# A decoder stack on one core: banks of an FFN chunk from one pool, read halfway by ScalarE; other slots, ranks and listed durations

## The chip, the cores and the metric

The kernel runs on one core of a Trainium2 chip, in one launch. The metric is device time in microseconds (us), the median over executions. The engines are named as the profile names them: PE is TensorE's matrix multiply and PEld its weight load, DVE is VectorE, ACT is ScalarE, POOL is GpSimd, SP is SyncE, which issues nearly all DMAs here.

## The reference

Two layers over x of 256 tokens and 2048 features, all in float32. A layer has three parts, each added to x:

```python
h = rms_norm(x, attn_norm_g[l]); proj = h @ w_in[l]              # 2048 -> 4688 columns
mixed = concat([ssd_mixer(...), mla_mixer(...)]) @ w_out[l]      # state-space scan and causal attention
x = x + mixed
x = x + memory_cross_attention(rms_norm(x), rms_norm(mem), ...)  # 4 heads, 256 memory tokens
h = rms_norm(x, ffn_norm_g[l])
x = x + (silu(h @ w_gate[l]) * (h @ w_up[l])) @ w_down[l]        # hidden 5632
```

The third part, the feed-forward part (FFN), is what most of the change is about.

## The kernel before, in words

Every float32 matmul is made of three in the fast format float32r. A weight tile of 256 rows and 512 columns ("unit", `raw`) is loaded, split into `hi` (ACT rounds it) and `lo` (DVE takes the remainder, raw - hi), and the product is xh·hi + xh·lo + xl·hi. `raw`, `hi` and `lo` are buffers of one tag, `w`, which has 20. PE holds 128 rows of x as its stationary operand and streams 512 columns of weights into one PSUM bank of 512 numbers.

The eight banks are two pools: `ps_acc`, tag "acc", has four and `ps_tp`, tag "tp", has four. `gemm` takes two acc banks, one for each half of the tokens. Transposes and small products use tp.

The FFN goes over 11 column chunks of 512 hidden columns. Chunk 0 is a plain gemm for gate and one for up. Chunks 1 to 10 go through `gate_up` (L1310): parts of the rows of gate and up are combined so that seven products of 18 matmuls and two blocks of 24 do what eight products of 24 would. Sums of weights (`b11 + b12` and the like) are made by DVE in place in `raw`, some by DMA that adds (`plus`, on POOL's queue). A chunk has four banks: `q` and `f` from acc, `cg` and `cu` from tp. q collects one product after another and is read three times on the way and once at the end. `seven_rows` makes the combined rows of x ahead of the FFN.

The two halves of a chunk's result are turned by a DMA transpose (`split_T_dma`, `turn`): the tile `gg` is copied in 16-bit halves to `hs`, transposed by DMA to `ht`, copied back into `whole` (L430: gg's own memory is used again), and split into a pair of tiles dh and dl, the rows for the down product. Chunks form sections [0], [1, 2], [3, 4], ... [9, 10]. After each chunk of a section a half of the previous section's down products is made: `down` (L1383) makes 512 columns of x at a time with `gemm` and adds both accumulators to x (`add_x`, L1174). So between chunk 1 and 2, and between 2 and 3, lie two down products of 24 matmuls each; between later chunks two of 48.

Tiles of 4 KB a partition are of the tag "b4", which has 22; those of up to 2 KB of the tag "s2", which has 6.

Nothing is issued in the order of the code. Each call is recorded (`Recorder.add`) with its dependences, and `issue` (L272) sets the order by a list schedule: it walks through time with a cost for each operation (`cost`, L244) and a lag until its result is seen, takes for each engine the operation that can start first, and among equals the one of lower rank. Rank is the place in the code plus `rec.bias`: weight splits have -400, the sums of weights (`add`, L1304) -425. A tile takes a slot of its tag when its first operation is listed; tiles of a tag are numbered in the order of the code. With a margin m for its tag (L1448), a tile before which `ahead` earlier ones are still without a slot may take one only if more than min(m, ahead) are free; with m = 0, if any is. Then the operations are issued in the listed order, and on the chip each engine keeps its own in that order and waits by semaphores.

In `issue` a recorded operation is made real at L374, so every instruction has that line in the profile and is known by its tiles.

Of the kernel before, what the change touches and what calls it, by code (L numbers as in the profile page):

```python
# [8 lines left out]
F32 = mybir.dt.float32  # L9
# [8 lines left out]
P = 128  # L18
S = 256
# [169 lines left out]
class Recorder:  # L189
# [3 lines left out]
    LAG = 0.35  # L193
    DMA_LAG = 2.0
    SECOND = 0.6
# [48 lines left out]
    def cost(self, engine, method, args, kw, writes, reads):  # L244
        n = max(v.free_size() for v in reads + writes) if reads or writes else 1
        if method == "dma_start_transpose":
            return 2.2, 1.6
        if method == "dma_start":
            if "accum_op" in kw:
                return 1.3, 8.0  # L250
            if engine == "SP":
                return n * 512 / 360e3, self.DMA_LAG
            return (1.1 if engine == "Pool" else 0.1), self.DMA_LAG + 0.6
        if engine == "PE":
            n = args[0].free_size()
            if method == "transpose":
                return 0.1075, self.LAG
            passes = 1 if args[1].tile.dtype == F32R else 4
            return max(passes * n / 2400 + 0.003, 0.107), self.LAG
        ptr = sum(0.07 for v in reads if v.free_size() == 1)  # L260
        if engine == "ACT":
            return 0.09 + n * 0.833e-3 + ptr, self.LAG
        if engine == "Pool" and kw.get("op") == ALU.pow:
            return 0.3 + n * 0.165, self.LAG
        if engine == "Pool":
            return 0.15 + n * 2.2e-3, self.LAG
        fast = not any(v.tile.psum for v in reads + writes) and method in ("tensor_copy", "tensor_scalar")
        if method == "reciprocal":
            n *= 8
        return 0.065 + n * (0.52e-3 if fast else 1.04e-3) + ptr, self.LAG  # L270

# [106 lines left out]
def hybrid_kernel(ctx: ExitStack, tc: tile.TileContext, const, vec, rows, x_in, x_tr, mem, mem_tr, positions, w_in, w_q_b,  # L378
# [110 lines left out]
    def load_unit(w, r0, c0, n, pieces=1):  # L489

        if not ahead and not asked:
            return ask(w, r0, c0, n, pieces)
        key = id(w), r0, c0
        while key not in asked or (ahead and len(asked) <= 2):
            first = ahead.pop(0)
            asked[id(first[0]), first[1], first[2]] = ask(*first, 512)
        return asked.pop(key)
# [4 lines left out]

    def ask(w, r0, c0, n, pieces=1):
        raw = wpool.tile([P, 2, n], F32, tag="w", name=nm("raw"), bufs=20)
        src = w[r0:r0 + 256, c0:c0 + n].rearrange("(k p) n -> p k n", p=P)
        for i in range(pieces):
            k = slice(2 // pieces * i, 2 // pieces * (i + 1))
            SP.dma_start(raw[:, k, :], src[:, k, :])
        return raw
# [650 lines left out]
    def mem_T(l):  # L1160
# [11 lines left out]
        return mT  # L1172

    def add_x(j, accs):  # L1174
        for t in range(NT):
            xs = x[j][:, t, :]
            V.tensor_add(xs, xs, accs[t])

# [124 lines left out]

    def add(out, a, b, do=V.tensor_add):  # L1304
        rec.bias -= 425
        for o, u, v in zip(out, a, b) if isinstance(out, list) else [(out, a, b)]:
            do(o, u, v)
        rec.bias += 425

    def gate_up(wg, wu, c, x1, half, full, rstd):  # L1310
# [6 lines left out]
        c0 = 512 * c  # L1317
        q, f = acc_tile(), acc_tile()
        cg, cu = tp_tile(), tp_tile()
        gg, uu = b4([P, NT, 512], "gg"), [s2([P, 512], "uu") for _ in range(NT)]  # L1320

# [10 lines left out]
        product(q, half["a11"], [h11])  # L1332
        A.copy(gg[:, 0, :], q)

# [5 lines left out]
        product(f, half["s1"], [h11])  # L1340
        A.copy(uu[0], f)

        b22 = load_raw(wu, 1536, c0, 512)
        add(b11, b11, b22)
        add(b12, b12, b22)
        product(cu, full["s4"], b22, start=True)
        h22 = load_unit(wu, 256, c0, 512)
        add(h11, h11, h22)
        add(h12, h12, h22)
        product(cu, half["s4"], [h22])  # L1350
        product(q, full["s2"], b11)
        plus(b11, wg, 1536, c0)
        product(q, half["s2"], [h11])
        add(uu[0], uu[0], q, V.tensor_sub)

# [5 lines left out]
        product(q, full["s3"], b12)  # L1361
        product(q, half["s3"], [h12])
        mm_chunk([cu, f], x1, load_w(wu, 512, c0, 512), 512, [False] * NT, [True, True], again=True)
        A.copy(uu[1], f)
        add(uu[1], uu[1], q, V.tensor_sub)
        add(uu[0], uu[0], cu)
        mm_chunk([cg, q], x1, load_w(wg, 512, c0, 512), 512, [False] * NT, [True, False], again=True)
        add(gg[:, 0, :], gg[:, 0, :], cg)
        A.activation(gg[:, 0, :], gg[:, 0, :], AF.Silu, scale=rstd[:, 0:1])

        product(q, full["a22"], b11)
        product(q, half["a22"], [h11], stop=True)
        A.activation(gg[:, 1, :], q, AF.Silu, scale=rstd[:, 1:2])
        for t in range(NT):
            V.scalar_tensor_tensor(gg[:, t, :], uu[t], rstd[:, t:t + 1], gg[:, t, :], op0=ALU.mult, op1=ALU.mult)
        return gg

    def ffn(l, xT, rstd):
# [19 lines left out]
        for sec in sections:  # L1398
            for i, c in enumerate(sec):
                if c == 0:  # L1400
                    ahead.extend((w, r + h, 0) for w in (wg, wu) for r in FULL for h in (0, 256))
                else:
                    ahead.extend((w, r, 512 * c) for w, r in (
                        (wg, 1024), (wg, 1280), (wg, 0), (wu, 1024), (wu, 1280), (wu, 0), (wu, 1536), (wu, 1792),
                        (wu, 256), (wg, 1536), (wg, 1792), (wg, 256), (wu, 512), (wu, 768), (wg, 512), (wg, 768)))
                if before:
                    n = DC // len(sec)
                    ahead.extend((wd, 512 * r + h, 512 * j) for j in range(n * i, n * (i + 1)) for r in before
                                 for h in (0, 256))
            before = sec  # L1410
        ahead.extend((wd, 512 * r + h, 512 * j) for j in range(DC) for r in before for h in (0, 256))
        before = None
        for sec in sections:
            hT = []
            for i, c in enumerate(sec):
                if c == 0:
                    xs = [lambda i, k, t: half[f"a{t + 1}{1 + k // 2}"][:, i, k % 2, :], x1]
                    xs += [lambda i, k, t, b=b: full[f"a{t + 1}{b}"][:, i, k, :] for b in (1, 2)]
                    ag = gemm(xs, wg, FULL, 0, 512)
                    hh = b4([P, NT, 512], "gg")  # L1420
                    for t in range(NT):
                        A.activation(hh[:, t, :], ag[t], AF.Silu, scale=rstd[:, t:t + 1])
                    au = gemm(xs, wu, FULL, 0, 512)
                    for t in range(NT):
                        V.scalar_tensor_tensor(hh[:, t, :], au[t], rstd[:, t:t + 1], hh[:, t, :], op0=ALU.mult,
                                               op1=ALU.mult)
# [20 lines left out]
    with tc.manual_schedule():  # L1447
        rec.issue({"b4": 6, "s2": 2, "tp": 0, "w": 99, "acc": 4})  # L1448

# [72 lines left out]
```

## Time and profile before

| | |
|---|---|
| median of 3 runs | 2264.48 us (2263.03 to 2264.68) |
| the profiled execution | 2267.05 us, of which its span is 2265.3 |
| busy, share of the span | PE 98%, PEld 81%, DVE 84%, ACT 66%, POOL 4% |
| mean granted clock of PE | 0.997 of full speed |
| DMA | 215 GB/s in the mean |

Matmuls overlap in the profile (a row lasts some 390 ns, the next starts 227 ns after it), so a busy PE is judged by its starts and by what it waits for. Waits are inferred from semaphores; a wait for several is put down to the one that came last.

### The profile page before, as it was taken

To read this page: it belongs to the slowest core of one execution; us is meant where nothing else is said; L and a number is where in the kernel's file an instruction comes from. 1 tells how busy PE (TensorE), PEld (TensorE's weight loads), DVE (VectorE), ACT (ScalarE), POOL (GpSimd) and SP (SyncE) were. 2 spreads that over 40 slices of the span, in tenths; PEclk is the share of its full clock that TensorE was granted. 3 is DMA by queue.
4 is the path that set the end of the run, shared out by engine and by line. 5 is a ranking of instruction groups with operands and counts; after the bars stand their busy time and mean duration, and the time that the engine had idled before them with its cause. 6 is when DMAs were issued, how large, how long until landed. Compare 5 with 4: busy or idle time off the path is not lost.

```text
span 2265.3 us, 29133 instructions
## 1 busy us (share of the span) xinstructions
PE 2222.9 (98%) x10118; PEld 1845.7 (81%) x10118; DVE 1910.6 (84%) x2568; ACT 1500.4 (66%) x2183; POOL 93.0 (4%) x78
## 2 busy tenths in 40 slices
PE   9999999998999999999999999999989999999999
PEld 9878878787888888888898788887878888888787
DVE  7898876789998999999778888857899999999894
ACT  7768666766766666676666686657666667666762
POOL 0001000000000000000000010000000000000000
PEclk9999999999999999999999999999999999999999
DMA  9866496676777777787777665856767777777773
GB/s 319 236 193 186 142 284 196 187 212 197 239 224 212 229 232 235 228 247 226 194 230 223 172 177 171 244 185 182 219 201 226 232 220 213 236 231 226 239 234 138
DMA packets 374515, 487.96 MB, mean 215 GB/s; under 512 B 145376, under 2 KB 168544, under 8 KB 374368
## 3 DMA queue, kind: packets, MB, share of 16 engines
q1 hardware_dynamic: 363456, 465.13, 65.1%
q0 software_dynamic: 10912, 20.98, 5.5%
q8 instruction: 79, 1.29, 0.2%
q14 instruction: 68, 0.56, 0.1%
HBM read 450.92 MB, written 2.10 MB: 200 GB/s over the span
## 4 chain that ended last, share of the span: by engine, by line
PE 71%; DVE 6%; DMA 5%; issue 2%; ACT 1%; SPq 0%; DVEq 0%; ACTq 0%
PE acc L374 59%; PE tp L374 13%; DVE lo L374 3%; DMA raw<-in_w_up_dram 1%; DVE raw L374 1%; DMA ht<-hs 1%; ACT hi L374 1%; DVE x L374 1%; DMA raw<-in_w_xv_dram 0%; DMA raw<-in_w_out_dram 0%; DMA raw<-in_w_in_dram 0%; DVE uu L374 0%; DMA raw<-in_w_gate_dram 0%; SPq L374 0%; DVE hTl L374 0%
## 5 line engine op out<-in xcount | busy, mean ns | idle before, releaser
L374 ACT CAST hi<-raw 128x1024 fp32r<-128x1024 f32 (+3 forms) x996 | 1002.7, 1034 | 559.9 <-PE acc L374 223.4
L374 DVE TENSOR_TENSOR lo<-raw,hi 128x1024 fp32r<-128x1024 f32 (+3 forms) x998 | 1167.9, 1200 | 177.3 <-ACT hi L374 125.2
L374 PE MATMUL acc<-hi,x 128*128 128x512 f32 x1392 | 373.1, 392 | 0.0
L374 PEld LDWEIGHTS acc<-hi,x 128*128 128x128 f32 x1392 | 263.4, 189 | 55.4
L374 PE MATMUL acc<-hi,xTh 128*128 128x512 f32 (+1 forms) x768 | 289.3, 377 | 0.0
L374 PE MATMUL acc<-hi,xTl 128*128 128x512 f32 (+1 forms) x768 | 289.1, 376 | 0.0
L374 DVE TENSOR_TENSOR raw<-raw,raw 128x1024 f32<-128x1024 f32 x200 | 239.2, 1221 | 50.7 <-DMA raw<-in_w_up_dram 50.2
L374 PE MATMUL acc<-hi,hTh 128*128 128x512 f32 x704 | 273.9, 389 | 0.0
L374 PE MATMUL acc<-hi,hTl 128*128 128x512 f32 x704 | 273.9, 389 | 0.0
L374 PE MATMUL acc<-lo,x 128*128 128x512 f32 x696 | 214.8, 394 | 13.2 <-DVE x L374 13.2
L374 PE MATMUL acc<-lo,xTh 128*128 128x512 f32 (+1 forms) x768 | 211.7, 378 | 6.0 <-DVE uu L374 4.2
L374 PE MATMUL acc<-lo,hTh 128*128 128x512 f32 x704 | 191.2, 390 | 1.3 <-DVE lo L374 1.3
L374 PEld LDWEIGHTS acc<-lo,xTh 128*128 128x128 f32 x768 | 140.6, 188 | 31.3 <-DVE uu L374 6.8
L374 PEld LDWEIGHTS acc<-lo,x 128*128 128x128 f32 x696 | 131.1, 190 | 42.5 <-DVE x L374 14.9
L374 PEld LDWEIGHTS acc<-hi,xTh 128*128 128x128 f32 x768 | 144.8, 189 | 23.2 <-issue 0.7
L374 PEld LDWEIGHTS acc<-hi,xTl 128*128 128x128 f32 x768 | 144.7, 188 | 23.1 <-issue 0.7
L374 PEld LDWEIGHTS acc<-lo,hTh 128*128 128x128 f32 x704 | 131.8, 188 | 30.1 <-DVE lo L374 3.0
L374 PEld LDWEIGHTS acc<-hi,hTh 128*128 128x128 f32 x704 | 132.1, 188 | 27.5
L374 PEld LDWEIGHTS acc<-hi,hTl 128*128 128x128 f32 x704 | 132.1, 188 | 27.4
L374 PE MATMUL tp<-hi,x 128*128 128x512 f32 x480 | 128.6, 390 | 0.0
L374 DVE TENSOR_TENSOR x<-x,acc 128x512 f32<-128x512 f32 x128 | 83.5, 682 | 32.5 <-PE acc L374 32.4
L374 PEld LDWEIGHTS tp<-hi,x 128*128 128x128 f32 x480 | 90.1, 188 | 19.2
(306 smaller groups left out, 2781.7 us busy)
## 6 DMA issues: line engine op xcount, KB each, us to landing
raw<-in_w_gate_dram SPq DMA_DIRECT2D x176, 512.0 KB, 4.9
raw<-in_w_up_dram SPq DMA_DIRECT2D x176, 512.0 KB, 4.5
raw<-in_w_down_dram SPq DMA_DIRECT2D x176, 512.0 KB, 5.4
raw<-in_w_in_dram SPq DMA_DIRECT2D x80, 512.0 KB, 4.4
raw<-in_w_out_dram SPq DMA_DIRECT2D x64, 512.0 KB, 4.5
raw<-in_w_gate_dram POOLq DMA_DIRECT2D x40, 512.0 KB, 7.5
raw<-in_w_in_dram SPq DMA_DIRECT2D x46, 368.0 KB, 4.5
raw<-in_w_kv_b_dram SPq DMA_DIRECT2D x16, 512.0 KB, 3.9
```

The costliest lines, as they stand in the source:

```text
L374: fn(*args, **kw)
```

## The change

Six things are changed together. In `gate_up` all four banks of a chunk are tp tiles; q is copied by ACT to uu after its second and third product, and DVE subtracts that copy from f, where before ACT copied f and DVE subtracted q. `gg` becomes two s2 tiles, so the turned copy `whole` has a b4 tile of its own. The loads of rows 0 to 255 of gate and up (h11, h12) of chunks 1 to 10 get b4 tiles in place of w tiles. The sums into x use `add`, with rank -425. The list schedule has other durations and another DMA lag. The margin of tp goes from 0 to 2.

```diff
-    DMA_LAG = 2.0
+    DMA_LAG = 2.8
...
-                return n * 512 / 360e3, self.DMA_LAG
+                return n * 512 / 330e3, self.DMA_LAG
...
-            return max(passes * n / 2400 + 0.003, 0.107), self.LAG
+            return max(passes * n / 2400 + 0.0135, 0.107), self.LAG
...
-            return 0.09 + n * 0.833e-3 + ptr, self.LAG
+            return 0.17 + n * 0.833e-3 + ptr + (0.19 if "accum_out" in kw else 0.0), self.LAG
...
-        return 0.065 + n * (0.52e-3 if fast else 1.04e-3) + ptr, self.LAG
+        return 0.13 + n * (0.52e-3 if fast else 1.045e-3) + ptr, self.LAG
...
-            asked[id(first[0]), first[1], first[2]] = ask(*first, 512)
+            asked[id(first[0]), first[1], first[2]] = ask(*first[:3], 512, 1, first[3:])
...
-    def ask(w, r0, c0, n, pieces=1):
-        raw = wpool.tile([P, 2, n], F32, tag="w", name=nm("raw"), bufs=20)
+    def ask(w, r0, c0, n, pieces=1, other=False):
+        raw = b4([P, 2, n], "raw") if other else wpool.tile([P, 2, n], F32, tag="w", name=nm("raw"), bufs=20)
...
+    def add(out, a, b, do=V.tensor_add):
+        rec.bias -= 425
+        for o, u, v in zip(out, a, b) if isinstance(out, list) else [(out, a, b)]:
+            do(o, u, v)
+        rec.bias += 425
+
     def add_x(j, accs):
...
-            V.tensor_add(xs, xs, accs[t])
+            add(xs, xs, accs[t])
...
-        q, f = acc_tile(), acc_tile()
-        cg, cu = tp_tile(), tp_tile()
-        gg, uu = b4([P, NT, 512], "gg"), [s2([P, 512], "uu") for _ in range(NT)]
+        q, f, cg, cu = (tp_tile() for _ in range(4))
+        gg, uu = [[s2([P, 512], n) for _ in range(NT)] for n in ("gg", "uu")]
...
         product(f, half["s1"], [h11])
-        A.copy(uu[0], f)
 
         b22 = load_raw(wu, 1536, c0, 512)
+        product(cu, full["s4"], b22, start=True)
         add(b11, b11, b22)
         add(b12, b12, b22)
-        product(cu, full["s4"], b22, start=True)
         h22 = load_unit(wu, 256, c0, 512)
+        product(cu, half["s4"], [h22])
         add(h11, h11, h22)
         add(h12, h12, h22)
-        product(cu, half["s4"], [h22])
         product(q, full["s2"], b11)
         plus(b11, wg, 1536, c0)
         product(q, half["s2"], [h11])
-        add(uu[0], uu[0], q, V.tensor_sub)
+        A.copy(uu[0], q)
+        add(uu[0], f, uu[0], V.tensor_sub)
...
         product(q, half["s3"], [h12])
+        A.copy(uu[1], q)
         mm_chunk([cu, f], x1, load_w(wu, 512, c0, 512), 512, [False] * NT, [True, True], again=True)
-        A.copy(uu[1], f)
-        add(uu[1], uu[1], q, V.tensor_sub)
+        add(uu[1], f, uu[1], V.tensor_sub)
...
-                    ahead.extend((w, r, 512 * c) for w, r in (
+                    ahead.extend((w, r, 512 * c) + ((1,) if r == 0 else ()) for w, r in (
...
-                split_T_dma(hc, lambda t: hh[:, t, :], None, hh.rearrange("p t (u s) -> p (t u) s", s=S), (A, V))
+                split_T_dma(hc, lambda t: hh[t], None, None, (A, V))
...
-        rec.issue({"b4": 6, "s2": 2, "tp": 0, "w": 99, "acc": 4})
+        rec.issue({"b4": 6, "s2": 2, "tp": 2, "w": 99, "acc": 4})
```

The remaining lines of the diff follow from gg being two tiles.

## Rows read from the trace of the kernel before

**Rows 1.** The page, part 1: busy us, share of the span, instructions.
```profile
PE 2222.9 (98%) x10118; PEld 1845.7 (81%) x10118; DVE 1910.6 (84%) x2568; ACT 1500.4 (66%) x2183; POOL 93.0 (4%) x78
```

**Rows 2.** Chain of waits, 786 to 850: start us, us, what.
```profile
790.79 4.08 PE acc L374 x18
```

**Rows 3.** Windows: stretch, busy us by engine, PE clock, DMA share, GB/s.
```profile
437.00:592.00 155.00, 146.95 (x639) 119.91 (x638) 137.35 (x143) 103.10 (x128) 6.60 (x5) 0.98 0.66 202
592.00:1060.00 468.00, 464.06 (x2035) 381.27 (x2036) 431.33 (x411) 316.48 (x345) 20.26 (x17) 1.00 0.75 231
...
910.17:971.67 61.50, 61.49 (x271) 50.87 (x272) 56.53 (x55) 40.46 (x46) 2.42 (x2) 1.00 0.74 231
```

**Rows 4.** Waits of PE, whole span: us in total, times, longest us.
```profile
PE acc L374 <- DVE x L374: 13.2, 4, 5.7
PE tp L374 <- DVE x L374: 5.2, 4, 2.3
PE tp L374 <- DVE lo L374: 4.8, 7, 1.2
PE acc L374 <- DVE uu L374: 4.2, 6, 1.3
PE acc L374 <- DVE lo L374: 3.1, 4, 1.8
```

**Rows 5.** Timeline of PE, first layer, start of chunk 2: start us, us, instructions.
```profile
531.19 0.39 PE L374 MATMUL acc<-hi,hTl 128*128 128x512 f32 x1
537.22 1.22 PE L374 MATMUL acc<-lo,x 128*128 128x512 f32 x2 [5.64 <-DVE x L374]
538.24 1.91 PE L374 MATMUL acc<-hi,x 128*128 128x512 f32 x4
539.94 1.05 PE L374 MATMUL acc<-lo,x 128*128 128x512 f32 x2
...
543.15 1.07 PE L374 MATMUL acc<-hi,x 128*128 128x512 f32 x4
```

**Rows 6.** Timeline of PE, second layer, start of chunk 2.
```profile
1658.60 0.39 PE L374 MATMUL acc<-hi,hTl 128*128 128x512 f32 x1
1664.70 1.22 PE L374 MATMUL acc<-lo,x 128*128 128x512 f32 x2 [5.71 <-DVE x L374]
...
1669.68 0.63 PE L374 MATMUL acc<-lo,x 128*128 128x512 f32 x2
```

**Rows 7.** Timeline of DVE, 526 to 560.
```profile
536.48 2.48 DVE L374 TENSOR_TENSOR x<-x,acc 128x512 f32<-128x512 f32 x4
542.81 2.36 DVE L374 TENSOR_TENSOR lo<-raw,hi 128x1024 fp32r<-128x1024 f32 x2 [3.85 <-PE acc L374]
```

**Rows 8.** Waits of all engines, 1657 to 1690.
```profile
DVE lo L374 <- PE acc L374: 3.5, 1, 3.5
```

**Rows 9.** Groups by line and form: busy us, mean ns, idle before.
```profile
L374 DVE TENSOR_TENSOR lo<-raw,hi 128x1024 fp32r<-128x1024 f32 x932 | 1108.2, 1221 | 153.1 <-ACT hi L374 105.6 <-PE acc L374 34.8 <-issue 3.5
L374 ACT CAST hi<-raw 128x1024 fp32r<-128x1024 f32 x930 | 950.6, 1051 | 525.4 <-PE acc L374 218.0 <-DMA raw<-in_w_up_dram 68.8 <-DMA raw<-in_w_down_dram 43.7
...
L374 DVE TENSOR_TENSOR uu<-uu,acc 128x512 f32<-128x512 f32 x40 | 27.2, 681 | 0.8 <-ACT uu L374 0.8
...
L374 ACT COPY uu<-acc 128x512 f32<-128x512 f32 x40 | 23.3, 582 | 7.1 <-PE acc L374 7.0
```

**Rows 10.** Waits of SP's queue, whole span.
```profile
SPq L374 <- PE acc L374: 885.0, 410, 9.2
```

**Rows 11.** Timelines of DVE, ACT and PE between chunk 6 and chunk 7.
```profile
821.95 0.75 DVE L374 SCALAR_TENSOR_TENSOR gg<-uu,rx_y,gg 128x512 f32<-128x512 f32 x1 [1.96 <-ACT gg L374]
832.58 2.18 ACT L374 COPY hs<-gg 128x512 uint16<-128x512 uint16 x4
839.59 0.62 PE L374 MATMUL acc<-lo,x 128*128 128x512 f32 x2
```

**Rows 12.** The page, part 6: DMA issues, KB each, us to landing.
```profile
raw<-in_w_gate_dram SPq DMA_DIRECT2D x176, 512.0 KB, 4.9
```

More of the change, by code (lines that the diff above doesn't have):

```diff
@@ L1302, in plus @@
             G.dma_start(raw[h], src, accum_op=ALU.add)
[L1304 to L1308, printed above, removed]
     def gate_up(wg, wu, c, x1, half, full, rstd):
         c0 = 512 * c
-        q, f = acc_tile(), acc_tile()
-        cg, cu = tp_tile(), tp_tile()
-        gg, uu = b4([P, NT, 512], "gg"), [s2([P, 512], "uu") for _ in range(NT)]
+        q, f, cg, cu = (tp_tile() for _ in range(4))
+        gg, uu = [[s2([P, 512], n) for _ in range(NT)] for n in ("gg", "uu")]
         def product(acc, d, raw, start=False, stop=False):
@@ L1332, in gate_up @@
         product(q, half["a11"], [h11])
-        A.copy(gg[:, 0, :], q)
+        A.copy(gg[0], q)
         b12 = load_raw(wu, 1024, c0, 512)
@@ L1362, in gate_up @@
         product(q, half["s3"], [h12])
+        A.copy(uu[1], q)
         mm_chunk([cu, f], x1, load_w(wu, 512, c0, 512), 512, [False] * NT, [True, True], again=True)
-        A.copy(uu[1], f)
-        add(uu[1], uu[1], q, V.tensor_sub)
+        add(uu[1], f, uu[1], V.tensor_sub)
         add(uu[0], uu[0], cu)
         mm_chunk([cg, q], x1, load_w(wg, 512, c0, 512), 512, [False] * NT, [True, False], again=True)
-        add(gg[:, 0, :], gg[:, 0, :], cg)
-        A.activation(gg[:, 0, :], gg[:, 0, :], AF.Silu, scale=rstd[:, 0:1])
+        add(gg[0], gg[0], cg)
+        A.activation(gg[0], gg[0], AF.Silu, scale=rstd[:, 0:1])
         product(q, full["a22"], b11)
         product(q, half["a22"], [h11], stop=True)
-        A.activation(gg[:, 1, :], q, AF.Silu, scale=rstd[:, 1:2])
+        A.activation(gg[1], q, AF.Silu, scale=rstd[:, 1:2])
         for t in range(NT):
-            V.scalar_tensor_tensor(gg[:, t, :], uu[t], rstd[:, t:t + 1], gg[:, t, :], op0=ALU.mult, op1=ALU.mult)
+            V.scalar_tensor_tensor(gg[t], uu[t], rstd[:, t:t + 1], gg[t], op0=ALU.mult, op1=ALU.mult)
         return gg
@@ L1419, in ffn @@
                     ag = gemm(xs, wg, FULL, 0, 512)
-                    hh = b4([P, NT, 512], "gg")
+                    hh = [s2([P, 512], "gg") for _ in range(NT)]
                     for t in range(NT):
-                        A.activation(hh[:, t, :], ag[t], AF.Silu, scale=rstd[:, t:t + 1])
+                        A.activation(hh[t], ag[t], AF.Silu, scale=rstd[:, t:t + 1])
                     au = gemm(xs, wu, FULL, 0, 512)
                     for t in range(NT):
-                        V.scalar_tensor_tensor(hh[:, t, :], au[t], rstd[:, t:t + 1], hh[:, t, :], op0=ALU.mult,
+                        V.scalar_tensor_tensor(hh[t], au[t], rstd[:, t:t + 1], hh[t], op0=ALU.mult,
                                                op1=ALU.mult)
```

## The prediction

> **What bounds the kernel now.** Part 1 of the page comes first: TensorE (PE) has a matmul under way for 98% of the span and VectorE (DVE) is busy for 84% [rows 1]. Busy PE says little by itself, since matmuls overlap, so I went to the chain of waits for its rate: 18 matmuls of 512 columns take 4.08 us, 226.7 ns each [rows 2]. A period of the feed-forward part (FFN), one column chunk of gate and up with its share of the down product, has 7 products of 18 matmuls, two blocks of 24, and two down products of 48: 174 + 96 = 270, or 61.2 us at that rate. A measured period is 61.50 us, with DVE busy for 56.5 of it [rows 3]. So PE sets the time, DVE follows at 92%, and the kernel can only gain where PE stands still.
>
> Where it stands is in the waits of PE: 13.2 us for x's sums before it may write an acc bank, 5.2 us for x's sums before transposes into tp banks, 7.9 us for weight remainders (lo), 4.2 us for the sums in uu [rows 4]. Of the 13.2 us, two waits have 5.64 and 5.71; they lie at the same place in the two layers, where chunk 2 wants its first bank [rows 5, 6]. More is lost behind them: matmuls start 425 ns apart (538.24 to 539.94 holds four), the lower of the clock's two levels, before the rate returns [rows 5]. The windows say the same: in 437 to 592 PE lacks 8 us of busy time and the mean granted clock is 0.98; the three times longer rest of that layer's FFN lacks 4 us, at 1.00 [rows 3].
>
> **The change part by part.** The sum is made against the profiled execution: 2267.05 us, of which 2265.3 are the span. The median shown is 2264.48, 2.6 below; that is subtracted at the end.
>
> *Banks.* Chunk 2's q and f waited because acc has four banks: chunk 1's q and f, and the down products j=0 and j=1, whose sums into x come last on DVE. With q, f, cg, cu all from tp, the chunk's first product needs chunk 1's q, read by a Silu more than 10 us earlier (two down products of 24 matmuls lie between). The bank wait goes at both places. Its price from starts: 531.19 to 537.22 is 6.03 us for one matmul, 5.8 lost; then 14 matmuls take 5.93 us where 3.17 would do, 2.8 lost; 8.6 together [rows 5]. In the second layer, 5.9, and 12 matmuls in 4.98 where 2.72 would do, 2.3; 8.1 together [rows 6]. That is 16.7 us, the upper end. What is late next? DVE was working up to and through x's four sums, and stood for 3.85 us only afterwards, when PE limped and freed no weight buffers [rows 7]; in the second layer for 3.5 [rows 8]. If PE doesn't stop, a DVE that sets the pace can win only that idle time: the lower end, 7.4 us. I take 12, the middle, because DVE is not far behind: no wait of PE for lo anywhere is longer than 1.8 us [rows 4]. The other x waits on acc, 13.2 - 5.6 - 5.7 = 1.9 us, go too [rows 4]. Minus 14.
>
> *Reading q halfway by ACT.* The six waits for uu (4.2 us) are of one kind: q's third reading was a subtraction that also needed f's end, so PE could not go on with q until f was finished, copied and subtracted [rows 4]. Now a copy by ScalarE (ACT) reads q right after its product, and the block of 24 matmuls into cu and f (5.44 us) covers it; the copy has 0.58 us, the DVE operation it replaces as reader 0.68 [rows 9]. The copies stay three a chunk, the subtractions too, so no engine gets more work. Behind the copy on ACT stands the next hi, which is wanted by DVE and then PE; before it can stand a hi that waits for a buffer. Bounds: minus 4.2, if all go, and plus 35, if no reading is covered (rival D); I take minus 4, since the covers are there now.
>
> Against this stands a rule of the Trainium skill, Perfetto Trace Analysis, section Matmuls: independent groups should rotate through banks, so that one's reading overlaps the next one's matmuls, and an accumulation group targets one bank. A chunk whose q is read three times in the middle does not rotate; by the rule each reading would be exposed. The row of waits shows that q's two DVE readings a chunk cost 4.2 us over twenty chunks now, since other banks' products lie between [rows 4]. What it would cost otherwise is rival D.
>
> *x's sums rank with the weights'.* Rank moves them before the queued lo operations; no instruction is added. It matters where norms wait for x: PE's 5.2 us in four waits for transposes, 1.3 each [rows 4]. x's own sums, 0.68 each by the like uu row [rows 9], stay in that path, so 0.5 to 1 is to be had each time; and a sum put in front of a lo that is wanted sooner costs 0.68. Between minus 4 and plus 1; I take minus 2.
>
> *Slots.* gg moves to two s2 tiles (six in all; uu has the other two of a chunk), h11 and h12 to the b4 pool, and the turned copy `whole` takes a b4 of its own. w gains two of 20 buffers; SyncE's queue waits 885 us in all for PE to free such buffers [rows 10], hidden while PE is busy, so I count nothing. b4 has 22 tiles: 13 hold x's rows through the FFN (half 4, full 7 once a21 is done, x1 2), four the hidden chunks of the last section, two the present one's first. At the end of chunks 4, 6 and 8 that leaves three: dh, dl and whole stand before hs, ht and the next chunk's h11 in the pool's order, and with the margin (6) a later tile may not take a slot unless more are free than tiles stand before it. The kernel before shows the shortage: gg is complete at 822.7 and hs, which needs a slot, starts only at 832.58, near the time when the first old hidden tiles come free (24 matmuls before 839.59) [rows 11]. So I expect h11's load no sooner than the last old hidden tile's release, at 839.59 [rows 11]. Landing 4.9 us, hi 1.05, lo 1.22 make 846.8; q wants it after 12 matmuls, at 842.3 [rows 9, 11, 12]. It is 4.5 us late, unless the list lets PE do the twelve matmuls of f and of cu that need no h: 24 x 226.7 = 5.44 us of cover. The list picks what can start first, so it should. Bounds at six boundaries: 0 to 27 us; I take 0.5 each, plus 3, since the cover exceeds the lateness by one and the list counts 4.4 us for a load that takes 4.9.
>
> *The durations, tp's margin, cu's place.* They change no work, only the order: with margin 2 a later tp tile leaves banks to earlier ones, and cu's products stand in the code ahead of sums that they don't need. A matmul goes from 216 to 226.8 ns in the list (measured 226.7), a DVE operation on 1024 elements from 1.13 to 1.20 us (1.22), ACT from 0.94 to 1.02 (1.05), a load from 3.5 to 4.4 us (4.9) [rows 2, 9, 12]. All come nearer to the rows. The waits they bear on are lo's 7.9 us [rows 4]; a reshuffled list can also lose elsewhere. Minus 8 to plus 8; I take 0.
>
> *Sum.* -14 - 4 - 2 + 3 = -17: 2250.1 for an execution like the profiled one, 2247.5 after the 2.6.
>
> **The rivals.**
>
> B: DVE takes over. Without the stop, lo's become late in chunks 1 to 3, and only DVE's idle time is won: -7.4 for the banks, -1 for the rest of x, -2 for uu, +1: -9.4, 2255. For it: before chunks 2 and 3 the down products have 48 matmuls instead of 96, so DVE has less time to catch up. Against: it had 17.6 us of idle time in the 155 of that stretch [rows 3].
>
> C, on the slower side: the b4 shortage. If PE keeps its order, q waits 4.5 us at each of six boundaries: 27 us against the 20 won, +7: 2271.5. It decides from 3.3 us a boundary. For it: the wait for hs above, and the many waits on SyncE's queue, where a load that waits holds those behind it [rows 10]. Against: f's and cu's products, which are free to go first.
>
> D: exposed readings. Sixty of 0.58 us are 35, less 20 won: +15, 2279.5. By the 4.2 us measured it is unlikely. The rule of Perfetto Trace Analysis in the Trainium skill speaks for it.
>
> E: the new order gives and takes the same, or h11 eats what the banks win: 2264.5, within 4.5 us (0.2%, about what a measurement of this kernel can tell from no change).
>
> **How the numbers follow.** Forecast 0.49, B 0.17, E 0.15, C 0.16, D 0.03. Faster by over 0.2% (below 2260): forecast and B, 0.66; within: E, 0.15; slower: C and D, 0.19. The forecast's own range is 2237 to 2255. Its lower bounds together (16.7 + 1.9 + 4.2 + 4 + 8 = 34.8) give 2229.7; upwards the range takes in E and half of C: 2230 to 2271.
>
> **What would show it.** Right: no PE wait for x of over 2 us at chunk 2, the clock at its upper level there, no PE wait for uu, periods of 61.3 to 61.8. B: new waits of PE for lo between chunk 1 and 3 with DVE busy over 95%. C: at the starts of chunks 5, 7, 9 waits of PE for lo, with a load of w_gate late before them. D: waits of PE's q product for ACT's copies. The forecast is wrong if PE's idle time moves into the mixer, or if chunk 2's bank wait had been hiding a DVE lag of its own size.

## The result and the profile after

The changed kernel takes 2281.32 us (median of 8 runs, 2275.99 to 2299.03), the kernel before beside it 2264.56: a ratio of 1.0081 [1.0054, 1.0107], slower by 0.8%. The forecast was 2247.5 (2230 to 2271), faster. The profiled execution has 2282.34 us, of which 2280.6 are the span.

The page, part 1, of the kernel after (compare [rows 1]): busy us, share of the span, instructions.

```profile
PE 2238.1 (98%) x10118; PEld 1859.3 (82%) x10118; DVE 1922.5 (84%) x2578; ACT 1486.4 (65%) x2173; POOL 86.6 (4%) x78
```

The same 10118 matmuls keep PE busy for 15 us longer: some run at the lower clock. The shares are within a point of those of before and do not say where. Windows laid at the same matmuls do: first mixer, its output projection, first FFN, second output projection, second FFN. The kernel before (stretch, length, busy us of PE, PEld, DVE, ACT, POOL with counts, PE clock, DMA share, GB/s):

```profile
1.00:225.20 224.20, 221.96 (x1101) 193.36 (x1102) 190.78 (x416) 165.60 (x306) 13.68 (x11) 1.00 0.78 234
225.20:332.70 107.50, 106.60 (x512) 88.48 (x511) 84.24 (x186) 68.94 (x144) 4.45 (x4) 1.00 0.70 211
...
434.20:1131.90 697.70, 685.71 (x3003) 562.74 (x3002) 625.24 (x635) 466.11 (x537) 26.86 (x22) 1.00 0.73 222
...
1354.00:1461.20 107.20, 106.33 (x509) 87.99 (x508) 88.87 (x191) 73.84 (x152) 3.28 (x2) 1.00 0.72 211
...
1561.30:2261.00 699.70, 685.68 (x3002) 562.03 (x3001) 610.79 (x598) 447.52 (x503) 25.95 (x21) 1.00 0.71 218
```

The kernel after, the same stages:

```profile
1.00:243.50 242.50, 234.12 (x1109) 203.05 (x1109) 191.40 (x412) 169.26 (x305) 7.82 (x11) 0.95 0.74 218
243.50:353.60 110.10, 107.61 (x504) 89.11 (x505) 85.33 (x186) 70.42 (x151) 4.37 (x4) 0.98 0.70 206
...
453.50:1150.20 696.70, 686.05 (x3002) 563.18 (x3002) 632.49 (x649) 459.54 (x531) 25.74 (x22) 1.00 0.75 222
...
1368.50:1482.80 114.30, 111.36 (x522) 92.26 (x522) 91.20 (x205) 76.36 (x165) 4.12 (x2) 0.97 0.68 198
...
1582.30:2276.30 694.00, 684.64 (x3000) 561.70 (x2999) 616.40 (x606) 440.17 (x499) 24.83 (x21) 1.00 0.72 218
```

The first mixer is 18.3 us longer, 12.2 of it PE's busy time (clock 0.95) and 6.1 standing; the output projections are 2.6 and 7.1 longer. The FFNs, where the whole gain of 17 was expected, are 1.0 and 5.7 shorter.

PE's waits, kernel after, whole span (compare [rows 4]): us in total, times, longest.

```profile
PE tp L374 <- DVE lo L374: 14.9, 12, 3.9
PE tp L374 <- DVE dec L374: 3.7, 1, 3.7
...
PE tp L374 <- ACT uu L374: 2.5, 2, 1.8
...
PE tp L374 <- DVE x L374: 1.1, 2, 0.8
```

The 13.2 us of acc banks waiting for x [rows 4] are gone, and 4.1 of the 5.2 of tp. In their place lo is late (tp's part 4.8 before, 14.9 now), and a new wait for the decays (dec) has appeared in the mixer. What held PE at chunk 2 is gone; the time came back, above all, in two other places.

**First place: the decays.** Timeline of PE, kernel after:

```profile
195.17 0.39 PE L374 MATMUL acc<-hi,kvaTl 128*128 128x512 f32 x1
199.27 6.71 PE L374 MATMUL tp<-xd,dec 128*128 128x64 f32 x32 [3.71 <-DVE dec L374]
```

Windows of the kernel before, and then of the kernel after, for the stretch behind it:

```profile
200.00:220.00 20.00, 19.57 (x107) 17.66 (x106) 18.24 (x49) 18.18 (x54) 3.37 (x2) 1.00 0.95 240
```

```profile
200.00:220.00 20.00, 19.74 (x82) 18.62 (x81) 11.16 (x25) 10.28 (x19) 0.00 (x0) 0.50 0.15 43
```

PE stood 3.71 us, then ran 32 matmuls of 64 columns in one piece, and the granted clock is at its lower level (0.50 of 2.4 GHz) for all 20 us: 82 matmuls instead of 107. Why was dec late? Timeline of ACT, kernel after:

```profile
171.28 1.09 ACT L374 ACTIVATE dec<-tp 128x512 f32<-128x512 f32 x2 [2.86 <-PE tp L374]
...
195.84 0.71 ACT L374 COPY hs<-kv 128x256 uint16<-128x256 uint16 x2
196.57 1.28 ACT L374 ACT_TABLE_LOAD   x1
197.86 2.71 ACT L374 ACTIVATE dec<-dec 128x512 f32<-128x512 f32 x5
```

The first inputs were there at 171; the Exps run 26 us later, behind casts and norms of later code. In the kernel before the table load begins at 168.73 and the Exps at 170.03. The list adds TABLE_LOAD (1.3 us) to the start of an Exp when it picks ACT's next instruction, so work that could start within 1.3 us kept winning; e3 below tries that.

**Second place: chunk 1 of each FFN.** Timeline of all engines, kernel after:

```profile
508.55 2.49 POOL L374 DMA_DIRECT2D raw<-in_w_gate_dram  x2 [23.70 <-DVE lo L374]
508.73 3.77 SPq L374 DMA_TRANSPOSE ht<-hs  x1
...
523.00 2.56 ACT L374 COPY whole<-ht 128x1024 uint16<-128x1024 uint16 x2 [6.84 <-DMA ht<-hs]
...
526.67 1.23 DVE L374 TENSOR_TENSOR hTl<-whole,hTh 128x1024 fp32r<-128x1024 f32 x1 [6.38 <-ACT hTh L374]
...
530.29 1.68 PE L374 MATMUL tp<-lo,xTh 128*128 128x512 f32 x4 [3.88 <-DVE lo L374]
```

Chunk 0's transposing DMA starts 0.2 us after POOL's first adding DMA. The DMA view, 508 to 525, kernel after (busy tenths and GB/s in 40 slices; issues with KB each and median us to landing):

```profile
DMA  8886595999999999999999969981999999999999
GB/s 217 284 289 227 152 195 16 107 188 178 102 69 56 78 75 36 33 45 83 45 40 26 60 20 31 41 42 23 137 173 205 192 246 217 251 260 270 270 255 255
...
raw<-in_w_gate_dram POOLq DMA_DIRECT2D x2, 512.0 KB, 16.0
...
ht<-hs SPq DMA_TRANSPOSE x1, 14.2
```

The same view of the kernel before, 485 to 502, where the transposing DMA is 7 us away from the adding ones:

```profile
raw<-in_w_gate_dram POOLq DMA_DIRECT2D x2, 512.0 KB, 6.9
...
ht<-hs SPq DMA_TRANSPOSE x1, 5.3
```

The DMA engines are busy, and move mostly 20 to 80 GB/s for 7 us. The transposed copy lands after 14.2 us instead of 5.3; ACT's queue waits for it at `whole` (6.84 us), DVE behind it at hTl (6.38), and PE at the end (3.88).

### The profile page after: what moved, and what is told of

The parts are those of the page before. It is cut to its first block, busy times and chain, and to the rows that moved or that the text cites. A ratio compares the mean times of both kernels' runs of the same rounds, so it can differ in the third digit from the quotient of the medians.

```text
span 2280.6 us, 29062 instructions
## 1 busy us (share of the span) xinstructions
PE 2238.1 (98%) x10118; PEld 1859.3 (82%) x10118; DVE 1922.5 (84%) x2578; ACT 1486.4 (65%) x2173; POOL 86.6 (4%) x78
## 5 line engine op out<-in xcount | busy, mean ns | idle before, releaser
L374 ACT CAST hi<-raw 128x1024 fp32r<-128x1024 f32 (+2 forms) x983 | 984.8, 1033 | 457.9 <-PE acc L374 124.5
L374 PE MATMUL tp<-hi,x 128*128 128x512 f32 x1680 | 449.3, 389 | 0.0
L374 PEld LDWEIGHTS tp<-hi,x 128*128 128x128 f32 x1680 | 315.5, 188 | 66.2
L374 PE MATMUL tp<-lo,x 128*128 128x512 f32 x840 | 260.8, 392 | 5.2 <-DVE lo L374 4.3
L374 PE MATMUL acc<-hi,xTl 128*128 128x512 f32 (+1 forms) x608 | 227.8, 375 | 0.0
L374 PE MATMUL acc<-hi,xTh 128*128 128x512 f32 (+1 forms) x608 | 226.7, 373 | 0.0
L374 PEld LDWEIGHTS tp<-lo,x 128*128 128x128 f32 x840 | 156.0, 188 | 43.8 <-DVE lo L374 8.9
L374 PEld LDWEIGHTS acc<-hi,xTl 128*128 128x128 f32 x608 | 114.8, 189 | 17.6 <-issue 1.7
L374 PE MATMUL tp<-hi,xTh 128*128 128x512 f32 x320 | 126.5, 395 | 0.0
L374 PE MATMUL tp<-hi,xTl 128*128 128x512 f32 x320 | 126.3, 395 | 0.0
L374 ACT COPY whole<-ht 128x1024 uint16<-128x1024 uint16 x51 | 66.4, 1355 | 84.9 <-DMA ht<-hs 84.9
```

Source lines behind the costliest of these rows:

```text
L374: fn(*args, **kw)
```

## Experiments

Ratios are to the kernel before, run beside each one on the same chip (2270 to 2272 there); 0.01 is 22.7 us. Theory M: the new durations lose the mixer. Theory F: the collision of DMAs holds the FFN. Later theory N: every list is a draw, that is, any change of a duration reorders it, for better or worse by chance. The letters S and D have their meaning in each expectation. Column two of the table is the first mixer with its output projection (first matmul to first matmul of the cross attention), column three both FFNs; both are from windows of each run's one profile. The profiled executions of e3, e12, e16 and e17 were 4 to 7 us above their median, that of e7 5 below. The kernel after was timed only with the result, beside a kernel before that took 2264.56; differences from it go by ratio here, and between the spans of the profiles they come out 3 to 14 us less favourable.

| kernel | ratio [95%] | mixer + out, layer 1 | FFNs |
|---|---|---|---|
| before | 1 | 331.7 | 1397.4 |
| e12 banks, reading alone on before | 0.9960 [0.9944, 0.9975] | 331.8 | 1393.0 |
| e1 after, old durations | 0.9869 [0.9856, 0.9882] | 332.3 | 1370.4 |
| e9 e1, q and f in acc | 0.9872 [0.9856, 0.9887] | 333.6 | 1368.6 |
| e17 e1, margin 0 | 0.9875 [0.9859, 0.9890] | 333.4 | 1375.6 |
| e11 e1, no rank | 0.9896 [0.9878, 0.9913] | 333.5 | 1376.3 |
| e18 e1, h in w | 0.9929 [0.9915, 0.9943] | 330.9 | 1383.1 |
| e16 e1, no adding in chunk 1 | 0.9948 [0.9931, 0.9964] | 332.0 | 1392.2 |
| e13 e1, DVE 60 ns | 0.9949 [0.9933, 0.9965] | 334.7 | 1376.5 |
| e10 e1, q read late | 0.9969 [0.9956, 0.9982] | 332.0 | 1389.1 |
| e2 before, new durations | 1.0086 [1.0070, 1.0102] | 353.7 | 1395.0 |
| after | 1.0081 [1.0054, 1.0107] | 352.6 | 1390.7 |
| e3 after, Exps early | 1.0063 [1.0043, 1.0083] | 345.8 | 1405.9 |
| e4 after, no adding in chunk 1 | 1.0026 [1.0016, 1.0037] | 351.9 | 1385.8 |
| e5 after, DVE old | 0.9984 [0.9973, 0.9994] | 341.8 | 1377.9 |
| e6 after, ACT old | 0.9997 [0.9985, 1.0008] | 343.2 | 1391.8 |
| e7 after, PE old | 1.0090 [1.0074, 1.0106] | 345.7 | 1395.6 |
| e8 after, loads old | 1.0024 [1.0014, 1.0033] | 345.5 | 1387.3 |
| e14 after, DVE 120 ns | 1.0003 [0.9992, 1.0014] | 344.7 | 1394.3 |
| e15 e3 and e4 together | 0.9985 [0.9973, 0.9997] | 349.4 | 1385.5 |

**e1: the changed kernel with the old durations.**

```
-    DMA_LAG = 2.8
+    DMA_LAG = 2.0
-                return n * 512 / 330e3, self.DMA_LAG
+                return n * 512 / 360e3, self.DMA_LAG
-            return max(passes * n / 2400 + 0.0135, 0.107), self.LAG
+            return max(passes * n / 2400 + 0.003, 0.107), self.LAG
-            return 0.17 + n * 0.833e-3 + ptr + (0.19 if "accum_out" in kw else 0.0), self.LAG
+            return 0.09 + n * 0.833e-3 + ptr, self.LAG
-        return 0.13 + n * (0.52e-3 if fast else 1.045e-3) + ptr, self.LAG
+        return 0.065 + n * (0.52e-3 if fast else 1.04e-3) + ptr, self.LAG
```

> The changed kernel with the list's old durations and DMA lag; banks, slots, ranks and margin stay new. Theory M (the new durations spoil the order in the first mixer: ACT's Exps of the decays are put off to 196.6 us, PE then waits 3.7 us and runs 20 us at the lower clock): the first mixer goes back from 242 to about 224 us, the whole to 2248 to 2262, the lower end if the DMA transposes and the adding DMAs of chunk 1 no longer fall together. Rival S (the slots in b4 and the halfway readings cost the time): it stays at 2275 or above, with the FFN no shorter than the 694 to 697 us of the changed kernel.

Measured: 2240.39 us (2237.96 to 2243.82), better than either theory had it and faster than both kernels. The five durations cost 42 us by the profiles (spans 2280.6 and 2239.0), 48 by the ratios. Windows of e1, first mixer and the two FFNs:

```profile
1.00:226.70 225.70, 223.06 (x1101) 193.25 (x1102) 190.70 (x416) 165.66 (x306) 13.66 (x11) 0.99 0.78 233
...
434.70:1121.10 686.40, 681.52 (x3002) 561.02 (x3001) 629.17 (x641) 458.36 (x530) 25.85 (x22) 1.00 0.76 225
...
1550.70:2234.70 684.00, 681.47 (x3000) 560.78 (x2999) 613.21 (x602) 440.93 (x499) 24.94 (x21) 1.00 0.74 221
```

The mixer is as before, and the FFNs are 11.3 and 15.7 us shorter: the gain that was forecast, and more, is there once the durations are out.

**e2: the durations alone**, on the kernel before (the five lines above the other way, and tp's margin 2).

```
-        rec.issue({"b4": 6, "s2": 2, "tp": 0, "w": 99, "acc": 4})
+        rec.issue({"b4": 6, "s2": 2, "tp": 2, "w": 99, "acc": 4})
```

> The kernel before with the new durations, DMA lag and tp margin alone; banks, slots and ranks stay old. Theory M: the first mixer is 18 us longer as in the changed kernel, and chunk 2's bank wait is still there: 2275 to 2290. Rival S: the durations are harmless, 2260 to 2268.

Measured: 2287.72 us, 1.0086. The first mixer takes 243.4 us, though of the other parts only tp's margin is in it, and e1, which has that margin too, takes 225.7: the loss there comes with the durations, not with banks or slots. The other half of the expectation failed: no acc bank waits for x over 1.6 us. In its place PE waits, once in each layer, for the turned chunk 0, whose transposing DMA starts 81 us into the FFN (51 in the kernel before). Waits of PE, e2:

```profile
PE acc L374 <- ACT hTh L374: 14.0, 2, 7.4
```

**e3: the Exps of the decays early**, by a smaller addition in the list.

```
-                        wait += self.TABLE_LOAD
+                        wait += 0.6
```

> The changed kernel, but the list holds a table load against an operation of ACT with 0.6 us instead of 1.3 when it chooses (the load's own time is still counted). Theory M: the Exps of the decays come before the work of later code, the first mixer is 18 us shorter, 2263 within 4, and the executions spread less than the changed kernel's 23 us because the clock no longer falls there. Rival: the Exps are not what delays PE, and it stays at 2281.

Measured: 2285.86 us, 1.0063; no gain clear of the intervals, where 18 us were expected. The table load now begins at 176.73, the decays go to PE in runs of 8 and 16, and in this stretch the clock holds. Windows of e3:

```profile
200.00:220.00 20.00, 20.00 (x111) 18.23 (x110) 16.98 (x41) 16.11 (x38) 3.67 (x2) 1.00 0.66 204
```

The first mixer is 14.8 us shorter (227.7). So the late Exps cost that stage 15 of its 18 us; but the output projection behind it grew from 110.1 to 118.1, and the FFNs by 15.3 together. In the output projection PE now waits for the turned result of the scan (ysTh), and the clock is 0.95; e1 has no wait of PE there and 1.00. Waits of PE, and then the window, of e3, 228.7 to 346.8:

```profile
PE acc L374 <- ACT ysTh L374: 3.7, 1, 3.7
```

```profile
228.70:346.80 118.10, 113.96 (x522) 93.98 (x523) 90.36 (x204) 73.09 (x158) 4.26 (x4) 0.95 0.68 200
```

DMA view of e3, 500 to 525, where both kinds of DMA start 0.17 us apart:

```profile
raw<-in_w_gate_dram POOLq DMA_DIRECT2D x2, 512.0 KB, 21.2
...
ht<-hs SPq DMA_TRANSPOSE x1, 19.3
```

And PE's timeline in e3 there:

```profile
526.78 2.07 PE L374 MATMUL tp<-lo,xTh 128*128 128x512 f32 x4 [8.12 <-DVE lo L374]
```

As close together as in the kernel after, the DMAs took a third longer, and PE waited twice as long (8.12 us, 3.88 there). What the mixer gained went here and into the output projection.

**e4: no adding DMAs in chunk 1**; DVE makes that sum there.

```
-        plus(b11, wg, 1536, c0)
+        if c > 1:
+            plus(b11, wg, 1536, c0)
...
         b21 = load_raw(wg, 1536, c0, 512)
+        if c == 1:
+            add(b11, b11, b21)
```

> The changed kernel, but chunk 1 adds b21 to b11 by DVE from the tile that is loaded anyway, instead of by two adding DMAs on POOL's queue: two DVE sums more (2.3 us) in a layer, two DMAs of 512 KB less. Theory F (in both layers chunk 0's transposing DMA and these adding DMAs start within 0.2 us of each other, and then every DMA takes 11 to 18 us): no DMA of the FFN over 10 us around chunk 1, the FFN 5 to 9 us shorter in each layer, the whole 2263 to 2271. Rival D (DVE is the bound there): no gain or 2 us a layer more, 2281 to 2286.

Measured: 2277.43 us, 1.0026, 12 us less than the kernel after by the ratios and 2.3 by the spans; the FFNs of the profile are 2.4 us a layer shorter, where theory F had 5 to 9. The collision is gone (the transposing DMA takes 5.1 us), but waits of PE stay in chunks 1 to 3 (3.0 us for uu; lo 5.5 in four). Theory F holds for a part at most.

**e15: e3 and e4 together**, to settle what ate e3's gain.

> The kernel of the third experiment (1.0063: first mixer 227.7, but FFNs of 702 and 704 us, where chunk 1's two adding DMAs and chunk 0's transposing one start within 0.2 us of each other and take 19 to 25 us), and in addition no adding DMAs in chunk 1: its third sum is made by VectorE. Theory F (the collision ate what the mixer gained): no DMA over 12 us near chunk 1, both FFNs about 692, 2260 to 2266, 0.995 to 0.999. Rival (the FFN's length is the order of weights and not the DMAs): FFNs stay over 698 and the time at 1.004 to 1.007.

Measured: 2269.31 us, 0.9985 against e3's 1.0063: 18 us, with FFNs 8.3 and 12.1 shorter. DMA view of e15, 500 to 525:

```profile
ht<-hs SPq DMA_TRANSPOSE x1, 4.9
```

Without the adding DMAs beside it the same transposing DMA takes 4.9 instead of 19.3 us, and PE's wait of 8.12 us is gone; the longest left in that FFN is 2.8. This part of theory F is shown. That all 18 us are the collision's is not: the edit also reorders the list, and e13 below moves as much without any DMA.

**e16: e4's edit on e1.**

> The kernel after with the old durations (0.987 of before), and no adding DMAs in chunk 1. There the transposing DMA starts 0.7 us before the first adding one, and takes 10 us, they 9 to 11. Theory F: a smaller collision goes, its price 1 to 3 us a layer; but VectorE, busy for 58 to 59 of 60 us in chunks 1 to 3, has one sum of 1.22 us more for each of two buffers: 0.985 to 0.988. Rival (VectorE's stretch is full and pays for both sums): 0.988 to 0.990.

Measured: 2259.07 us, 0.9948: 18 us worse than e1, more than either side expected. In e1 the transposing DMA starts 0.7 us before the adding ones and lands after 10.1; ACT waits 1.2 for it. There is little to win, and DVE has two sums of 1.22 us more a layer. That alone is not 18 us, and the rest stays open; e13 below shows that a mere reordering can be as large.

**e5 to e8: one old duration at a time**, each one line of e1's diff (e8 the two of the loads).

> The kernel after, with only VectorE's old durations in the list (0.065 us plus 1.04 ns an element); all other durations, banks, slots and margins as after. All five together are worth about 40 us (2281 after, 2240 with the old ones). Theory S (one duration carries it, and it is VectorE's: with 1.20 us for a lo the list sees an engine that is nearly full, and puts weights and decays off): about 2245, first mixer about 226 us, each FFN about 686. Theory N (every list is a draw: a changed duration reshuffles it, and no single one carries the loss): between 2250 and 2285, and the stages move independently of one another.

> The kernel after, with only ScalarE's old durations (0.09 us plus 0.833 ns an element, no term for accum_out). Theory S: about 2280, as VectorE's carries the loss; but if ScalarE's does (the late Exps of the decays run on it), first mixer 226 instead of 242 and 2262. Theory N: in this list no run of more than eight decay matmuls stands in the first mixer, so that its 18 us go and the clock does not stay low there; the FFNs keep their 696 and 694 or move by some us either way: 2255 to 2275.

> The kernel after, with only TensorE's old duration (216.3 instead of 226.8 ns for 512 columns). Theory S: about 2280, unless TensorE's carries the loss. Theory N: this list still has 26 decay matmuls in one run in the first mixer, and has them in the second one too: first mixer about 242 us, second about 235 instead of 218, 2280 to 2300, whatever the FFNs do.

> The kernel after, with only the loads' old durations (3.46 instead of 4.39 us for a load in the list). Theory S: about 2280. Theory N: no run of more than eight decay matmuls, so the first mixer is about 226 us; but loads are asked for too late by the list's reckoning, measured ones take 4.9 us: the FFNs' waits for lo stay or grow; 2260 to 2285.

Measured: 2268.91, 2270.88, 2292.55 and 2276.50 us; against the kernel after 22 and 19 less, 2 more, 13 less. No one duration carries the loss. Stages move independently: with DVE's old duration the second mixer takes 231.0 us, though it has 218.4 in the kernel after and 219.8 in e1. What the four were expected to do in single stages came half true (e6 223.4 and e8 229.0 in the first mixer where 226 were expected; e7 234.1, not 242, and 223.3 in the second, not 235).

**e13 and e14: changes that mean nothing by themselves.**

```
-        return 0.065 + n * (0.52e-3 if fast else 1.04e-3) + ptr, self.LAG
+        return 0.06 + n * (0.52e-3 if fast else 1.04e-3) + ptr, self.LAG
```

and in the kernel after 0.12 for 0.13.

> The kernel after with the old durations (0.987 of before), but VectorE's constant 0.060 instead of 0.065 us: a change of 0.4% in one duration, that means nothing by itself. Theory N (each list is a draw): the order changes and the time moves by 5 us or more to either side, 0.982 to 0.998. Theory D (the old durations as a set keep the mixers' and FFNs' order, the new ones break it): within 5 us, 0.985 to 0.989, first mixer 224 to 228 us, FFNs 683 to 689.

> The kernel after (1.008 of before), but VectorE's constant 0.120 instead of 0.130 us: 0.8% of one duration. Theory N: the run of 26 decay matmuls in the first mixer is broken up by this change (runs of eight), so that stage falls from 242 to about 226 us, and the FFNs move by some us to either side: 0.996 to 1.004. Theory D: the new durations cost their 40 us in any such list: 1.004 to 1.012.

Measured: 2260.30 (0.9949) and 2272.24 us (1.0003): 5 ns in one duration cost 18 us (19 by the spans), 10 ns won 18 (10 by the spans). e13's loss is spread: 6 us in the FFNs, 5 in the first cross attention, 5 in the second mixer. In e14 the first mixer falls to 226.8, as expected, and the output projection grows to 117.9, as in e3. A change that means nothing thus moves the time as theory N says. From these two I estimate that any edit that reorders the list is measured with an uncertainty of some 18 us, beside which the interval of its timing is small.

**e9 to e12, e17, e18: parts of the change undone in e1, or done alone.**

```
e9   -        q, f, cg, cu = (tp_tile() for _ in range(4))
     +        q, f = acc_tile(), acc_tile()
     +        cg, cu = tp_tile(), tp_tile()
e10  -        A.copy(uu[0], q)
     -        add(uu[0], f, uu[0], V.tensor_sub)
     +        add(uu[0], uu[0], q, V.tensor_sub)
     ...
e11  -            add(xs, xs, accs[t])
     +            V.tensor_add(xs, xs, accs[t])
e17  "tp": 2 -> "tp": 0
e18  - + ((1,) if r == 0 else ())
e12  before, with e9's and e10's edits the other way
```

> The kernel after with the old durations (2240, 0.987 of before), but a chunk's q and f from the acc pool as before; reading halfway, rank, slots and margin stay. By the prediction's term for the banks (12 to 17 us, two x waits at chunk 2 and what the lower clock adds) it should be 2252 to 2257, 0.994, with waits of PE for x of 5 to 6 us at chunk 2 of each layer. Rival: the reading halfway frees q and f early enough that the pool no longer matters: 2240, 0.987, and no x wait over 2 us.

> The kernel after with the old durations (0.987 of before), but q is read by the subtraction again, after f's copy, and f is copied as before; the banks stay in one pool. By the prediction's term (4 us) 2244, 0.989, with six waits of PE for uu of 0.7 us. Rival: with all four from one pool a late reading also holds the next chunk's banks: 2250 to 2265, 0.992 to 0.998.

> The kernel after with the old durations (0.987 of before), but x's sums in program order again. By the prediction's term 2242, 0.988 (2 us). Rival: the rank is what brings x's sums to chunk 2's bank and to the norms in time, and carries a good part of the 30 us: 2252 or more, 0.993.

> The kernel before with two edits alone: q and f from tp, and q read halfway by ScalarE. By the prediction's terms (14 + 4) 0.992 of before, and what is left to 0.987, some 11 us, is rank, slots and margin. Rival: these two carry it all, 0.987. Rival: in the old slots it gives nothing, since weights wait for buffers: 0.998 to 1.002.

> The kernel after with the old durations (0.987 of before), and tp's margin 0 as before: what is left of the change is one pool, the reading halfway, rank, slots and cu's place. By the prediction (margin at nothing): 0.985 to 0.989. Rival (a draw of the list's order, as for 0.060 us of VectorE's constant, which gave 0.995): outside that, 0.980 to 0.998.

> The kernel after with the old durations (0.987 of before), but h11 and h12 ask for buffers of w again, not of b4. By the prediction's term for the slots (b4 short at chunks 5, 7 and 9, 3 us lost) it should be a little faster, 0.985 to 0.987. Rival: w's two more buffers let loads start earlier in the stretch of chunks 1 to 3, where VectorE has no time to spare, and are worth 5 to 12 us: 0.989 to 0.993.

Measured: e9 2241.15, e10 2263.19, e11 2246.83, e12 2261.31, e17 2241.71, e18 2254.40 us. Waits of PE in e9, all that name x:

```profile
PE tp L374 <- DVE x L374: 2.5, 2, 1.4
```

With q and f back in acc there is still no wait of acc for x. The timelines put it down to the rank of x's sums. PE makes the two down products ahead of chunk 2 from 521.2 to 532.1 in e9, and from 522.3 to 533.2 in e11, which lacks the rank. Timelines of DVE, e9 and then e11:

```profile
526.41 1.28 DVE L374 TENSOR_TENSOR x<-x,acc 128x512 f32<-128x512 f32 x2
...
532.15 1.28 DVE L374 TENSOR_TENSOR x<-x,acc 128x512 f32<-128x512 f32 x2
```

```profile
573.48 1.87 DVE L374 TENSOR_TENSOR x<-x,acc 128x512 f32<-128x512 f32 x3
```

With the rank the sums run as soon as each product is done and free its banks; in the kernel before all four ran after the second one [rows 7]. Without it they come 40 us late, and PE does not wait either, since chunk 2's banks are tp's. So pool or rank, either one, does for chunk 2; rank alone, on the kernel before, was not tried. Waits of PE in e10, with the banks in one pool and the late reading:

```profile
PE tp L374 <- DVE lo L374: 15.2, 14, 2.7
PE tp L374 <- DVE uu L374: 4.9, 6, 1.5
```

The six waits for uu are back, as expected; lo's eight further waits (14 for 6 in e1, 10.4 us more) were not foreseen by the prediction's term, but the rival's range has the time. With all else as in e1, reading is worth 23 us, the h slots 14, rank 6, pool and margin at most 1.4; all but the first lie within a draw's 18, and the first not far above. Reading was not tried without the pool. Pool and reading alone (e12) give 9, between what its expectation and its second rival said.

DVE's busy time goes with these FFN numbers. Windows of 180 us, from 60 us into the first FFN (chunks 1 to 3), e1 first:

```profile
495.00:675.00 180.00, 177.06 (x776) 144.78 (x775) 173.52 (x167) 128.78 (x142) 7.20 (x6) 1.00 0.81 240
```

The kernel before:

```profile
494.00:674.00 180.00, 172.85 (x748) 141.64 (x747) 168.98 (x162) 123.08 (x136) 8.29 (x7) 0.98 0.75 222
```

The kernel after:

```profile
513.00:693.00 180.00, 170.66 (x730) 138.32 (x729) 162.18 (x156) 120.36 (x132) 7.20 (x6) 0.98 0.78 220
```

And e3:

```profile
505.00:685.00 180.00, 165.47 (x707) 134.19 (x706) 157.02 (x152) 117.08 (x129) 4.80 (x4) 0.97 0.81 217
```

In these four PE's count and DVE's busy time fall together: 776 matmuls with 173.5 us, 748 with 169.0, 730 with 162.2, 707 with 157.0. That alone does not say which holds which, since every weight unit brings DVE its lo and PE its matmuls. And the tie is loose in others. e11:

```profile
494.00:674.00 180.00, 176.01 (x772) 144.28 (x771) 169.71 (x163) 126.02 (x139) 7.17 (x6) 1.00 0.79 236
```

e15 has 742 matmuls with the same 169.7. In e1 DVE is busy for 96% of this stretch, so it is likely, and not shown, that DVE is the limit there. What is shown is the chain of the kernel after: a DVE that stands for the transposing DMA, then PE for lo. Behind this stretch, in the kernel after:

```profile
693.00:1113.00 420.00, 418.93 (x1844) 345.42 (x1843) 389.04 (x380) 273.64 (x301) 15.35 (x13) 1.00 0.76 233
```

PE is busy for 418.93 of 420 us there. There is nothing left to win there.

## Why the prediction was wrong

*The failed step* is "The durations, tp's margin, cu's place. They change no work, only the order ... I take 0", with bounds of 8 us to either side. The durations cost 42 to 48 us (e1). Two things were wrong in it. That all durations "come nearer to the rows" was taken as harmless; but the list turns durations into an order and not into time. And the bounds were drawn from the waits for lo that stood in the trace, 7.9 us: that a reshuffled list "can also lose elsewhere" is said there and given no price, while the 3.71 us for the decays and the 20 us at the lower clock arose where no wait had been. The table separates two parts of the loss. First mixer and output projection take 331 to 335 us in all ten lists with the old durations (e13's 5 ns aside), and 342 to 354 in all ten with at least three of the five new: 7 to 23 us that come with the durations as such. The FFNs of the whole changed structure take 1370 and 1377 with the old ones (e1, e13) and 1378 to 1406 with the new (the kernel after, e3, e5 to e8, e14); with a part of the change undone the old reach 1392 (e16). So how much of the FFNs' loss comes with the durations and how much is a draw stays open. The collision of DMAs is the largest piece found there (20 us in the FFNs between e3 and e15), and not the only one: e7, whose transposing DMA starts 43 us after the adding ones, takes 1395.6. Late Exps are shown to be 15 us of the mixer (e3), but curing them moved half of it into the output projection, to a wait for ysTh and the lower clock. Why the new durations put that work late is not settled.

*Banks and reading* (-14 and -4 forecast). Right that the two bank waits would go, and that no wait for x would stand at chunk 2; with the old durations (e1) the lower clock behind them is gone too. The FFNs of e1 are 27 us shorter, where banks, reading and slots together were put at -15. What the prediction missed is that the rank frees chunk 2's banks without the pool (e9), so that the pool adds nothing that is seen beside it; by e10 the reading halfway is worth far more than 4 us, as far as one draw tells. The rival D, exposed readings, for which the rule of Perfetto Trace Analysis in the Trainium skill, section Matmuls, was taken to speak, did not come: q's readings cost PE 2.5 us in two waits in the kernel after, not 35.

*Rank* (-2): 6 by e11, within a draw, and beside the pool; it was looked for only at the norms. *Slots* (+3, rival C): wrong in sign as far as e18 tells; there is no wait of PE at chunks 5, 7 and 9, where 693 to 1113 has PE busy for all but 1.1 us. So the b4 shortage did not decide; that f's and cu's products went first, as was argued against C, is not shown. *cu's place* was not tried alone, nor were gg's slots.

*Rival B* (DVE takes over, 2255) is half borne out. Its sign was new waits for lo with DVE over 95% busy. The kernel after has the waits with DVE at 90%; e1 has DVE at 96% (173.5 of 180 us, 169.0 before) with waits for lo of 7.2 us, no longer than the 7.9 of before. *Rival E* came out in e14, by compensation and so by luck.

*What would have shown it* was named: "The forecast is wrong if PE's idle time moves into the mixer". It did, yet no case carried it in the chances: the slower side (0.19) was all slots and readings.

The version to keep is the change without its durations: 2240.4 us, 0.987 of the kernel before. Since 5 ns in one duration moves it to 0.995, it is a good draw as much as a good structure; e17, the same with margin 0, gives 0.9875.

## What to carry to other kernels

A scheduler's durations are a seed as much as a model: price them apart from the structural edits, run a few neighbouring values to see the spread, and keep the order that runs best, not the durations that are truest. Where the second engine is busy for most of a stretch, look at what it waits for as well: in the kernel after DVE's 6.38 us became PE's 3.88. Before a reorder, list which DMAs of different kinds can now start together.

## What the runs showed of the hardware

Where a transposing DMA started within 0.2 us after an adding one, every DMA issued beside them in the next 10 us was slow: the transposing one took 14.2 us to landing in the kernel after and 19.3 in e3 instead of 4.9 to 5.3, the plain loads 13.9 to 15.6 and 15.8 to 17.6 instead of 4.9, with the DMA engines busy at mostly 20 to 80 GB/s in the kernel after. Where it started 0.7 us before them (e1) it took 10.1. The Trainium skill, Advanced Engine Details and Errata, section DMA Advanced Topics, says that transposing DMAs on trn2 are as fast as regular ones; the traces agree for one away from adding DMAs (5.3 beside 4.9 for a load [rows 12]) and not beside them. Why the two disturb each other no run here shows.

The granted clock fell to its lower level at 199.7, when PE had stood 3.71 us and begun, 0.4 us before, 64-column matmuls in one piece, and stayed there for 20 us. In e3 the same matmuls went in runs of 8 and 16 between wide ones, with no such stop before them, and the level stayed the upper one in 200 to 220; which of the two made the difference is not separated. The eight executions of the changed kernel spread over 23 us (2275.99 to 2299.03), the four of e1 over 6 (2237.96 to 2243.82).
